# A two-layer decoder step: the second layer's S5 matrices built during the first layer's FFN, and S5 steps admitted by an account of VectorE's queue

## The chip, the cores and the metric

The kernel runs on one core of one Trainium2 chip. The metric is the device time of one execution in microseconds (us). TensorE is written PE here, VectorE DVE, ScalarE ACT, GpSimd POOL and SyncE SP, as the profile writes them.

## What is computed

Two layers (DEPTH 2), each over 288 tokens (256 of a prompt and 8 x 4 samples) of width 2048, cut from the reference:

```python
z = x @ w_in                                  # 2048 -> 3072: u (1024), cv (1024), cg (1024)
y5, h_re, h_im = _s5(u, h0_re, h0_im, ...)    # 64 groups x 16 channels, 64 complex states, a scan over positions
g5 = gelu(y5);  s5_out = g5 * sigmoid(g5 @ s5_w_glu)
c = cv * sigmoid(cg); c = causal_dwconv(c, width 31); c = silu(LN(c))
x = LN(ALPHA * x + concat(s5_out, c) @ w_out)
hup = causal_dwconv(x @ ffn_w_up, width 3);  gate, val = split(hup)
x = LN(ALPHA * x + (silu(gate) * val) @ ffn_w_down)
x = LN(ALPHA * x + sigmoid(x @ pe_w_gate) * (p @ pe_w))
```

Inside `_s5` the input matrix depends on weights alone: `bb = q * b` with q a complex number for each state, and powers of the state's factor `ab` times `c` give the output matrices. None of it depends on x.

## The kernel before

All large products run as three PE passes on 128x128 weight blocks (high part times high part, low times high, high times low; `run`, L369, L374, L375), one block after another in one fixed list. Every 8 blocks are one transfer of 512 KB (`wraw`, issued by SP). ACT makes the high part (`whi`, L195) and DVE the low part (`wlo`), two units of 8 blocks ahead of PE. A layer's phases are, in blocks: u0 (64), p0 to p7 (32 each, with v1 to v4 of 16 each after p1 to p4), g (64), o (256), then the FFN (up0, dn0, up1, dn1, up2, dn2) and the gate pg.

The S5 mixer works in 8 chunks of 8 groups beside the phases u0 to g of its own layer. For chunk c: `em` (the input matrix, built by four DVE operations in `make_e` from `sbt` and `sqb`) multiplies the inputs `ust` on PE (`inject`, output tile `bu`); DVE scans (`scan`, with tables `stb` and `sd` that POOL makes in `tables`); PE projects (`project`, tile `y`) with `om` and `tm`; `gelu` writes `y_d` to DRAM and `u<-y_d` brings it back as the input of phase g. `make_o` builds `om` from powers `pw`, and, through a PE product `kps`, a tile `kp`, a store `k_d` and a load `tm<-k_d`, the short-range matrix `tm`. `om` and `tm` of chunk c+1 wait for the projection of chunk c.

The convolution module runs beside it: after p_j, DVE fills `cbuf`, POOL stores it (`cb_d`), loads four shifted copies (`stack`), writes `cbuf` out (`out_dram<-cbuf`) and loads the next `cbuf`, which has one buffer. The convolution of stage j runs on PE after p_(j+1). In g, the first 32 blocks go by k, so that the block of k = 7 needs chunk 7 (`xs_g`, split to `xh` and `xl`).

Each engine executes its own queue in the order written. The S5 generators are asked for another step at every second block (`tick`). How far they may go is set by `self.rate` and by a clock `pe_t` that adds a fixed price for each block (369 ns), convolution tap (640 ns) and so on; a wait such as `wait(PJ_LAG)` counts on that clock. In `xs_g` the steps left are forced out, whatever the clock says.

```python
self.scan[2] = min(self.scan[2] + self.rate * (self.pe_t - self.pe_l), BANK)
while self.scan and self.scan[2] > 0 and self.step(self.scan): pass
...
while k not in gsplit:          # xs_g
    self.step(scan); self.run_timed(True); split_g(True)
```

## Time and profile before

| | us |
|---|---|
| three timed runs: median (lowest to highest) | 2794.82 (2787.64 to 2795.36) |
| the profiled execution | 2793.7 |
| its span, first to last instruction | 2791.9 |
| PE busy in it | 2684.0 (96%) |
| DVE, ACT, POOL busy | 1815.6, 1353.2, 304.3 |

PE is the engine that sets the time: every us in which it waits, or runs at its lower clock, is in the result, and other engines count only where PE waits for them. In the profile's slices PE is at 90% or more almost everywhere except in the two mixers, which lie at 0 to 300 us and at 1380 to 1680 us.

### The profile page before, as it was taken

The page shows a single profiled execution, that of the slowest core. Times are in us where ns is not written, and L with a number is a line of the kernel's source. Part 1 is how long each engine was busy: PE and PEld are TensorE (multiplying, and loading weights), DVE is VectorE, ACT ScalarE, POOL GpSimd, SP SyncE. Part 2 cuts the span into 40 slices and gives each one's busy share as a digit, 9 for nine tenths or more (in the row PEclk, how much of TensorE's full clock was granted, in tenths as well). Part 3 has the DMA queues.
Part 4 walks back from the last instruction along what each step waited for, and adds up shares of the span by engine and source line. Part 5 has one row for each costly group of instructions (what it writes and reads, how often), then busy time and mean ns, then how long its engine had stood idle before and what let it go on. Part 6 is the DMA issues. An engine that isn't in the chain of part 4 may idle for free. (4 is left out here: it accounts for less than half of the span.)

```text
span 2791.9 us, 57891 instructions
## 1 busy us (share of the span) xinstructions
PE 2684.0 (96%) x23696; PEld 2623.0 (94%) x23696; DVE 1815.6 (65%) x3017; ACT 1353.2 (48%) x2224; POOL 304.3 (11%) x923
## 2 busy tenths in 40 slices
PE   8889999999999999999889879999999999999997
PEld 7778999999999999999888769999999999999997
DVE  6875768664566456667778747676645664566686
ACT  3444547553455345536454435475534553455363
POOL 3442001000000000000115410010000000000000
PEclk9999999999999999999999999999999999999998
DMA  7887544554455544544468874445555455455543
GB/s 238 240 237 224 171 152 164 162 181 163 158 168 164 180 159 157 181 162 151 145 197 242 225 206 156 150 161 165 180 166 162 159 179 171 150 173 171 166 152 102
DMA packets 175609, 487.72 MB, mean 175 GB/s; under 512 B 37616, under 2 KB 61696, under 8 KB 175344
## 3 DMA queue, kind: packets, MB, share of 16 engines
q1 hardware_dynamic: 160832, 434.56, 48.6%
q0 software_dynamic: 14512, 49.47, 6.4%
q8 instruction: 186, 3.05, 0.4%
q14 instruction: 79, 0.65, 0.1%
HBM read 463.27 MB, written 20.68 MB: 173 GB/s over the span
## 5 line engine op out<-in xcount | busy, mean ns | idle before, releaser
L369 PE MATMUL acc<-xh,whi 128*128 128x288 f32 x4656 | 1389.3, 299 | 13.0 <-ACT xh L528 5.1
L374 PE MATMUL acc<-xl,whi 128*128 128x288 f32 x4357 | 1289.7, 296 | 0.6 <-DVE xl L140 0.2
L375 PE MATMUL acc<-xh,wlo 128*128 128x288 f32 x4357 | 1284.3, 295 | 0.5 <-issue 0.5
L195 ACT ACTIVATE whi<-wraw 128x1024 fp32r<-128x1024 f32 x766 | 791.4, 1050 | 350.5 <-PE acc L374 220.4
L140 DVE TENSOR_TENSOR wlo<-wraw,whi 128x1024 fp32r<-128x1024 f32 x766 | 918.6, 1223 | 28.6 <-issue 12.5
L369 PEld LDWEIGHTS acc<-xh,whi 128*128 128x128 f32 x4656 | 876.5, 188 | 20.5 <-ACT xh L528 5.4
L374 PEld LDWEIGHTS acc<-xl,whi 128*128 128x128 f32 x4357 | 821.4, 189 | 3.7 <-DVE xl L140 2.1
L375 PEld LDWEIGHTS acc<-xh,wlo 128*128 128x128 f32 x4357 | 823.8, 189 | 0.7 <-issue 0.7
L140 DVE SCALAR_TENSOR_TENSOR fo<-fe,parf,fo 128x304 f32<-128x304 f32 x352 | 188.2, 535 | 354.2 <-ACT fo L1250 347.9
L369 PE MATMUL acc<-hh,whi 128*128 128x288 f32 x1408 | 416.4, 296 | 0.0
L374 PE MATMUL acc<-hl,whi 128*128 128x288 f32 x1312 | 387.7, 296 | 0.0
L375 PE MATMUL acc<-hh,wlo 128*128 128x288 f32 x1312 | 387.4, 295 | 0.0
L369 PEld LDWEIGHTS acc<-hh,whi 128*128 128x128 f32 x1408 | 264.9, 188 | 0.1
L375 PEld LDWEIGHTS acc<-hh,wlo 128*128 128x128 f32 x1312 | 247.2, 188 | 0.0
L374 PEld LDWEIGHTS acc<-hl,whi 128*128 128x128 f32 x1312 | 247.0, 188 | 0.0
L1246 ACT ACTIVATE fe<-acc 128x256 f32<-128x256 f32 x176 | 67.6, 384 | 301.1 <-PE acc L375 301.1
L1256 POOL COPY fstage<-fe 128x9 f32<-128x9 f32 x176 | 42.2, 240 | 1035.3 <-ACT fe L1247 1024.5
L428 ACT ACTIVATE ln_q<-x 128x288 f32<-128x288 f32 x90 | 40.2, 446 | 221.0 <-DVE x L140 221.0
L140 DVE TENSOR_TENSOR x<-x,acc 128x288 f32<-128x288 f32 x64 | 29.1, 454 | 144.7 <-PE acc L375 144.7
L1250 ACT ACTIVATE fo<-fe,parf 128x304 f32<-128x304 f32 x176 | 113.0, 642 | 16.5
L1270 ACT ACTIVATE hh<-fth 128x288 fp32r<-128x288 f32 x88 | 39.2, 445 | 162.9 <-DVE fth L140 162.9
L140 DVE SCALAR_TENSOR_TENSOR x<-x,acc 128x288 f32<-128x288 f32 x64 | 29.0, 453 | 132.9 <-PE acc L375 132.9
(237 smaller groups left out, 2366.9 us busy)
## 6 DMA issues: line engine op xcount, KB each, us to landing
wraw<-in_wts_dram SPq DMA_DIRECT2D x776, 512.0 KB
stack<-cb_d POOLq DMA_DIRECT2D x56, 282.0 KB, 8.8
cw<-in_convw_dram POOLq DMA_DIRECT2D x16, 512.0 KB, 5.7
cbuf<-in_convi_dram POOLq DMA_DIRECT2D x16, 283.5 KB, 4.5
cb_d<-cbuf POOLq DMA_DIRECT2D x16, 283.5 KB, 4.0
out_dram<-cbuf POOLq DMA_DIRECT2D x16, 283.5 KB, 10.4
tm<-k_d SPq DMA_DIRECT2D x64, 64.0 KB
sbt<-in_s5b_dram SPq DMA_DIRECT2D x14, 256.0 KB
```

Of the source, the lines that this page charges most:

```text
L140: return f(out, *args, **kw)
L195: self.nc.scalar.activation(hi, self.raw[s], AF.Copy)
L369: nc.tensor.matmul(out, w[0], xh, start=first, stop=False)
L374: nc.tensor.matmul(out, w[0], xl, start=False, stop=False)
L375: nc.tensor.matmul(out, w[1], xh, start=False, stop=last)
L428: nc.scalar.activation(st["q"], v, AF.Square)
L1246: nc.scalar.activation(e[:, 2:2 + SEQ], acc[:, :SEQ], AF.Copy)
L1250: nc.scalar.activation(o[:, :w], e[:, 2:EW], AF.Identity, bias=self.prm("ffn_conv_b", m), scale=self.prm("ffn_conv_w2", m))
L1256: nc.gpsimd.tensor_copy(stage[:, z, :, 0], e[:, SEQ:EW:6])
L1270: nc.scalar.activation(hh[i], h, AF.Copy, scale=0.5)
```

## The change

In short: (1) `s5_early` builds the second layer's S5 matrices while the first layer's FFN runs, from dn0 on, and stores them in DRAM (`se`, `so`, `sk`); the second mixer loads them instead of building them. (2) An S5 step is admitted while the account of DVE's work (`dve_c`, 150 ns + 1.05 ns per element, twice that for the scan) is less than 1600 ns ahead of `pe_t`, in place of the rate. (3) Products are placed by that account: `e` is ready at `dve_c + E_LAG`, projections and `kps` wait until `dve_c + D_LAG` in place of `PJ_LAG`. (4) `pe_t` counts 400 ns for a block and 500 for a tap. (5) In the second layer a small POOL copy from `x32[0]` stands ahead of POOL's first S5 work.

```diff
-RATE = (1.05, 0.9)
-SETUP_RATE = 3
-BANK = 1400.0
+BACKLOG = 1600.0
+E_LAG = 2500.0
+K_LAG = 10000.0
+D_LAG = 1000.0
-PJ_LAG = 6000.0
+EARLY_LAG = 7000.0
+EARLY_RATE = 0.5
...
-            self.core.dve_t += 70.0 + n / 0.96
+            cost = 150.0 + (2.1 if name == "tensor_tensor_scan" else 1.05) * n
+            self.core.dve_c = max(self.core.dve_c, self.core.pe_t) + cost
...
-            self.scan[2] = min(self.scan[2] + self.rate * (self.pe_t - self.pe_l), BANK)
-            while self.scan and self.scan[2] > 0 and self.step(self.scan):
+            while self.scan and self.dve_c - self.pe_t < BACKLOG and self.step(self.scan):
...
-                self.pe_t += 369.0
+                self.pe_t += 400.0
...
+    def s5_load(self, l, c, pool, eng, which):
...
+    def s5_into(self, m, bt, qb):
+
+        V = self.V
+        shp = [P, 4, 2, ST]
+        V.tensor_tensor(m, qb, bt[:, :, 0:1].to_broadcast(shp), OP.mult)
+        V.tensor_tensor(qb, qb, bt[:, :, 1:2].to_broadcast(shp), OP.mult)
+        yield 1.0
+        V.tensor_tensor(m[:, :, 0], m[:, :, 0], qb[:, :, 1], OP.subtract)
+        V.tensor_tensor(m[:, :, 1], m[:, :, 1], qb[:, :, 0], OP.add)
+        yield 1.0
+
+    def s5_out(self, l, c, cc, bc, pw, bs, work):
...
+    def s5_steps(self, bs, pw, kp):
+
+        nc = self.nc
+        kps = self.ps.tile([P, 512], F32, tag="one", name="kps", bufs=1)
+        self.pe_t += 400.0
...
+    def s5_early(self, l, pool):
...
+        for c in range(S5C):
+            bt, qb = [self.s5_load(l, c, pool, eng, w) for w in "bq"]
+            cc, bc = self.s5_load(l, c, pool, eng, "o")
+            yield 1.0
+            yield from self.wait(EARLY_LAG)
+            m = work([P, 4, 2, ST])
+            yield from self.s5_into(m, bt, qb)
...
+            yield from self.wait(EARLY_LAG)
+            eng.dma_start(ed, m)
+            yield from self.s5_out(l, c, cc, bc, pw, bs, work)
+            yield from self.wait(EARLY_LAG)
+            self.s5_steps(bs, pw, kp)
+            eng.dma_start(od, pw[:, :, :, 1:5])
+            yield 1.0
+            yield from self.wait(EARLY_LAG)
...
+            eng.dma_start(kd, kp.rearrange("p k g o -> p (k g o)"))
+            self.early[c] = (ed, od, kd)
...
+            if early:
+                e = mp.tile([P, 4, 2, ST], F32, name="sbt", tag="sbt", bufs=1)
+                eng.dma_start(e, early[c][0])
+                return (e,)
...
+            if early:
+                kd, pk = early[c][2], cc
+            else:
+                yield from self.s5_out(l, c, cc, bc, pw, bs, work)
+                yield from self.until(self.dve_c + D_LAG)
...
-            self.at(BACK_LAG, back)
+            self.at(2000.0 if early else K_LAG, back)
...
-                state["e"] = c
+                self.timed.append((self.dve_c + E_LAG, lambda c=c: state.update(e=c)))
...
         def tail(c, us):
-            yield from self.wait(PJ_LAG)
+            yield from self.until(self.dve_c + D_LAG)
...
+        go0 = load_o(0, nc.gpsimd)
+        bt0 = None if early else self.s5_load(l, 0, mp, nc.gpsimd, "b")
+        if l:
+            G.tensor_copy(kp[:, 0, 0, 0:1], self.x32[0][:, 0:1])
...
-                    self.pe_t += 640.0
+                    self.pe_t += 500.0
...
+                if h == 0 and l + 1 < DEPTH:
+                    pre = self.start(self.s5_early(l + 1, fp), EARLY_RATE)
                 self.run(ph[f"dn{h}"], lambda k: (hh[k - j0], hl[k - j0]), ev_d0 if h == 0 else ev_dn)
```

`s5_load`, `s5_out` and `s5_steps` hold what `load_b`, `load_e`, `load_o` and `make_o` held. In the FFN, `eng` is SP.

Where instructions stand is decided by these accounts. Three places follow, each before and after.

The first is PE near the end of the first layer's mixer: the last projection `y` (chunk 7), before.

```order
L1108 MATMUL acc<-stack,cw 32x32 x4
L389 MATMUL y<-ust,tm 32x72 x4
L389 MATMUL y<-hin,om 32x72 x8
...
L389 MATMUL y<-hin,om 32x72 x8
L1105 MATMUL acc<-stack,cw 32x256 x4
L1108 MATMUL acc<-stack,cw 32x32 x4
L369 MATMUL acc<-xh_87,whi 128x288
```

It stands in the convolution ahead of p7. In the changed kernel it stands in g, between k = 6 (`xh_101`) and k = 7 (`xh_102`, which is made from this very chunk):

```order
L375 MATMUL acc<-xh_101,wlo 128x288
L389 MATMUL y<-ust,tm 32x72 x4
L389 MATMUL y<-hin,om 32x72 x8
...
L389 MATMUL y<-hin,om 32x72 x8
L369 MATMUL acc<-xh_102,whi 128x288
L374 MATMUL acc<-xl_118,whi 128x288
```

It moved 60 blocks later, and nothing is left between it and the block that needs it. Chunk 7's `kps` stands 14 blocks ahead of it.

The second is the same projection of the second layer. Before, it stands in p7, after 22 of its 32 blocks:

```order
L375 MATMUL acc<-xh_92,wlo 128x288
L389 MATMUL y<-ust,tm 32x72 x4
L389 MATMUL y<-hin,om 32x72 x8
...
L389 MATMUL y<-hin,om 32x72 x8
L369 MATMUL acc<-xh_93,whi 128x288
```

In the changed kernel it stands in the convolution ahead of p7, 22 blocks earlier:

```order
L1194 MATMUL acc<-stack,cw 32x32 x4
L389 MATMUL y<-ust,tm 32x72 x4
L389 MATMUL y<-hin,om 32x72 x8
...
L389 MATMUL y<-hin,om 32x72 x8
L1191 MATMUL acc<-stack,cw 32x256 x4
```

The third is POOL's queue where the second layer begins. Before, S5 comes first of all, and the convolution's transfers follow later:

```order
L745 DMA h_16275<-in_h_dram 128x512
L1038 MEMSET bsm 128x256
L1039 MEMSET kp 128x96
L1040 MEMSET hin 128x8
L790 DMA scc<-in_s5c_dram 128x128
L792 DMA sbc<-in_s5bs_dram 128x128
L776 DMA sbt<-in_s5b_dram 128x512
L1002 MEMSET om 128x1024
L886 TENSOR_TENSOR stb<-tix,fint 128x288
```

In the changed kernel the account admits no S5 step until after p0, and POOL has the first stage's transfers and the load of the second `cbuf` ahead of it:

```order
L1164 DMA stack<-cb_d 32x4x564 x4
L1166 DMA out_dram<-cbuf 128x567
L1201 DMA cbuf<-in_convi_dram 128x567
L866 DMA h_17177<-in_h_dram 128x512
L906 DMA sqb<-so_d_7902 128x512
L1125 COPY kp<-x_0_71 128x1
L1126 MEMSET bsm 128x256
L1127 MEMSET kp 128x96
L1128 MEMSET hin 128x8
L898 DMA sbt<-se_d_7901 128x512
L1085 MEMSET om 128x1024
L966 TENSOR_TENSOR stb<-tix,fint 128x288
```

On PE the first `bu` of the second layer follows 16 matmuls of the first convolution, 22 blocks later than before. POOL's tables of the second chunk now stand behind the load of the third `cbuf` (before: ahead of it), and in the first layer POOL's first tables stand behind the load of the second `cbuf` as well. The eight `kps` products of the second layer stand in dn0, up1 and dn1 of the first layer's FFN, 112 blocks apart.

## Rows read from the trace of the kernel before

**Rows 1.** Windows: us A:B, length, busy us of PE, PEld, DVE, ACT, POOL, clock, DMA

```profile
600.00:1220.00 620.00, 620.00 (x4652) 619.89 (x4651) 355.57 (x500) 289.57 (x444) 30.00 (x182) 1.00 0.52 167
1440.00:1680.00 240.00, 202.17 (x3298) 181.29 (x3299) 164.37 (x283) 98.38 (x189) 83.91 (x154) 0.92 0.80 223
```

**Rows 2.** PE's waits in 0 to 330 us: total, times, longest

```profile
PE bu L389 <- ACT em L815: 8.4, 7, 3.6
PE bu L389 <- DMA ust<-u_d: 6.0, 2, 3.4
...
PE y L389 <- DMA sqb<-q_d: 5.7, 1, 5.7
...
PE bu L389 <- issue: 1.6, 1, 1.6
```

**Rows 3.** PE's waits in 1360 to 1700 us

```profile
PE y L389 <- DMA wraw<-in_wts_dram: 7.6, 1, 7.6
...
PE lnp L510 <- DVE ln_dg L140: 7.2, 1, 7.2
PE y L389 <- ACT kp L858: 6.4, 2, 3.5
PE bu L389 <- DMA ust<-u_d: 5.2, 1, 5.2
PE acc L369 <- ACT xh L528: 5.1, 1, 5.1
PE y L389 <- DMA tm<-k_d: 3.1, 1, 3.1
PE bu L389 <- ACT em L815: 3.0, 3, 2.5
```

**Rows 4.** PE in order of time, second mixer: start, us, operation, wait before it

```profile
1455.53 1.08 PE L1105 MATMUL acc<-stack,cw 128*32 128x256 f32 x8 [7.40 <-DMA stack<-cb_d]
...
1485.37 1.21 PE L389 MATMUL bu<-ust,em 128*32 128x72 f32 x64
...
1580.38 2.15 PE L389 MATMUL bu<-ust,em 128*32 128x72 f32 x64 [5.17 <-DMA ust<-u_d]
...
1640.25 0.47 PE L389 MATMUL y<-ust,tm 128*32 128x72 f32 x8 [7.62 <-DMA wraw<-in_wts_dram]
```

**Rows 5.** DVE in order of time: the LayerNorm chain ahead of the second layer

```profile
1381.43 0.16 DVE L140 TENSOR_SCALAR ln_ne<-lnp 96x6 f32<-96x6 f32 x1 [1.85 <-PE lnp L459]
...
1387.70 0.87 DVE L140 SCALAR_TENSOR_TENSOR ln_dg<-ident,ln_n 96x288 f32<-96x288 f32 x1
```

**Rows 6.** DVE in order of time: the last LayerNorm's chain

```profile
2771.83 0.16 DVE L140 TENSOR_SCALAR ln_ne<-lnp 96x6 f32<-96x6 f32 x1 [1.78 <-PE lnp L459]
...
2774.36 0.45 DVE L140 SCALAR_TENSOR_TENSOR ln_dg<-ident,ln_n 96x288 f32<-96x288 f32 x1
```

**Rows 7.** POOL in order of time, 1380 to 1457 us

```profile
1383.61 0.68 POOL L886 TENSOR_TENSOR stb<-tix,fint 128x288 int32<-128x288 int32 x1
...
1444.53 0.56 POOL L1080 DMA_DIRECT2D out_dram<-cbuf  x1
1456.28 0.56 POOL L1115 DMA_DIRECT2D cbuf<-in_convi_dram  x1 [11.19 <-DMA out_dram<-cbuf]
```

**Rows 8.** The chain that ended last, 1640 to 1670 us: start, us, what

```profile
1649.15 3.19 DMA cb_d<-cbuf
...
1652.91 7.66 DMA stack<-cb_d
...
1660.59 7.21 DMA u<-y_d
...
1668.41 0.61 PE acc L369
```

**Rows 9.** DVE's groups by shape, 1400 to 1660 us: busy, mean ns, idle before

```profile
L140 DVE TENSOR_TENSOR sw<-scc,aP 128x512 f32<-128x512 f32 x16 | 10.7, 701 | 11.0 <-DMA scc<-in_s5c_dram 9.1 <-ACT em L815 1.9
...
L140 DVE TENSOR_TENSOR sw<-sqb,sbt 128x512 f32<-128x512 f32 x8 | 6.9, 867 | 17.3 <-DMA sqb<-q_d 9.1 <-DMA wraw<-in_wts_dram 8.2
```

**Rows 10.** PE's groups by shape, 1400 to 1680 us

```profile
L853 PE MATMUL kps<-pw,bsm 128*32 128x64 f32 x128 | 3.4, 224 | 0.0
```

**Rows 11.** DMA issues: queue, count, KB each, us to landing

```profile
y_d<-yw POOLq DMA_DIRECT2D x16, 144.0 KB, 3.5
...
sbt<-in_s5b_dram POOLq DMA_DIRECT2D x2, 256.0 KB, 4.9
```

**Rows 12.** ACT in order of time: one chunk's two `em` copies

```profile
1432.34 1.34 ACT L815 ACTIVATE em<-sw,mask 128x512 f32<-128x512 f32 x2 [3.87 <-DVE sw L140]
```

More of the change, by code (lines that the diff above doesn't have):

```diff
@@ L171, in __init__ @@
         self.nblk = DEPTH * NBLK
+        self.early = {}
     def stream_dma(self, upto):
@@ L281, in step @@
             return False
-        b[2] -= self.dve_t - t if b is self.scan else cost
+        b[2] -= cost
         return True
@@ L721, in stack_tile @@
         return mp.tile([P, 4, STW], F32, tag="stack", name="stack", bufs=1)
+    def s5_load(self, l, c, pool, eng, which):
+        a = self.a
+        if which == "b":
+            bt = pool.tile([P, 4, 2, ST], F32, name="sbt", tag="sbt", bufs=1)
+            eng.dma_start(bt, a["s5b"][l, c])
+            return bt
+        if which == "q":
+            qb = pool.tile([P, 4, 2, ST], F32, name="sqb", tag="sqb", bufs=1)
+            for q in range(4):
+                w = self.qd[l * NPAIR + 4 * c + q].rearrange("s g w -> (s g) w")
+                src = bass.AP(tensor=w.tensor, offset=w.offset, ap=[[P, 8], [0, CIN], [1, P]])
+                eng.dma_start(qb[:, q].rearrange("p i s -> p (i s)"), src)
+            return qb
+        cc = pool.tile([P, 4, 2, CIN], F32, name="scc", tag="scc", bufs=1)
+        eng.dma_start(cc, a["s5c"][l][:, 4 * c:4 * c + 4])
+        bc = pool.tile([P, 4, 2, CIN], F32, name="sbc", tag="sbc", bufs=1)
+        eng.dma_start(bc, a["s5bs"][l][:, 4 * c:4 * c + 4])
+        return cc, bc
@@ new lines, in s5_steps @@
+    def s5_steps(self, bs, pw, kp):
+        nc = self.nc
+        kps = self.ps.tile([P, 512], F32, tag="one", name="kps", bufs=1)
+        self.pe_t += 400.0
+        for i in range(2):
+            for q in range(4):
+                nc.tensor.matmul(kps[32 * q:32 * q + 32, :4 * CIN], bs[:, q, i].rearrange("p g c -> p (g c)"),
+                                 pw[:, q, i, 0:4].rearrange("p k o -> p (k o)"), start=(i == 0), stop=(i == 1),
+                                 tile_position=(0, 32 * q))
+        kv = kps[:, :4 * CIN].rearrange("p (k o) -> p k o", o=CIN)
+        for g in range(2):
+            nc.scalar.activation(kp[:, 3:7, g], kv, AF.Copy, scale=self.mask2[:, g:g + 1])
@@ L800, in load_u, with make_e @@
             return us
-        def make_e(bt, qb):
-            m = work([P, 4, 2, ST])
-            shp = [P, 4, 2, ST]
-            V.tensor_tensor(m, qb, bt[:, :, 0:1].to_broadcast(shp), OP.mult)
-            V.tensor_tensor(qb, qb, bt[:, :, 1:2].to_broadcast(shp), OP.mult)
-            yield 1.0
-            V.tensor_tensor(m[:, :, 0], m[:, :, 0], qb[:, :, 1], OP.subtract)
-            V.tensor_tensor(m[:, :, 1], m[:, :, 1], qb[:, :, 0], OP.add)
-            yield 1.0
+        def make_e(c, bt, qb=None):
+            m = bt
+            if not early:
+                m = work([P, 4, 2, ST])
+                yield from self.s5_into(m, bt, qb)
             mf = m.rearrange("p q i s -> p (q i) s")
@@ new lines, in make_o @@
+        def make_o(c, cc, bc=None):
+            if early:
+                kd, pk = early[c][2], cc
+            else:
+                yield from self.s5_out(l, c, cc, bc, pw, bs, work)
+                yield from self.until(self.dve_c + D_LAG)
+                while state["y"]:
+                    yield None
+                state["k"] = True
+                self.s5_steps(bs, pw, kp)
+                self.at(PS_LAG + 500.0, lambda: state.update(k=False))
+                yield None
+                k0 = kp[:, 3].rearrange("p g o -> p (g o)")
+                V.scalar_tensor_tensor(k0, self.eye, self.prm("s5_d", c), k0, op0=OP.mult, op1=OP.add)
+                kd = self.dp.tile([P, 7 * 2 * CIN], F32, tag="k_d", name="k_d", bufs=2)
+                G.dma_start(kd, kp.rearrange("p k g o -> p (k g o)"))
+                pk = pw[:, :, :, 1:5]
@@ L970, in gelu @@
             self.at(BACK_LAG, back)
-        state = {"i": -1, "p": -1, "e": -1, "o": -1, "y": False, "k": False}
+        early = self.early
+        state = {"i": -1, "p": -1, "e": -1, "o": -1, "y": False, "k": False, "t": -1}
         finals = []
@@ L1011, in main @@
                 yield from self.wait(PS_LAG)
+                while state["t"] < c:
+                    yield None
                 yield from scan(c, v, tb)
@@ L1025, in tail @@
         def tail(c, us):
-            yield from self.wait(PJ_LAG)
+            yield from self.until(self.dve_c + D_LAG)
             while finals:
@@ L1292, in ffn @@
                 nc.gpsimd.dma_start(a["ffno"][l][:, j0:j0 + n].rearrange("p j g b t -> p (j g) b t"), stage[:, :2 * n])
+                if h == 0 and l + 1 < DEPTH:
+                    pre = self.start(self.s5_early(l + 1, fp), EARLY_RATE)
                 self.run(ph[f"dn{h}"], lambda k: (hh[k - j0], hl[k - j0]), ev_d0 if h == 0 else ev_dn)
+                if last and l + 1 < DEPTH:
+                    assert pre not in self.bg
                 j0 += n
```

142 lines of the change are left out of this document (66 added, 76 removed).

## The prediction

> **What bounds the kernel now.** I read the busy time by stretches first, then PE's waits in each mixer, then the queues behind those waits. In the FFN PE is busy for 620.00 of 620 us at clock 1.00; in the second mixer it is busy for 202.17 of 240 us at a mean clock of 0.92 [rows 1]. So PE bounds the program, and only the mixers have time to give. From the FFN window a matmul takes 620 / 4652 = 0.133 us, so a block of three takes 0.40 us; I use that for every count of blocks. DVE is no bound: 164 of 240 us in the mixer, 356 of 620 in the FFN.
>
> PE's waits in the first mixer that S5 causes are 8.4 for `em`, 6.0 for `ust`, 5.7 and 1.6: 21.7 us [rows 2]. In the second mixer I count 7.6, 7.2, 6.4, 5.2, 5.1, 3.1 and 3.0 [rows 3] and 7.4 for the first `stack` [rows 4]: 45.0 us. The reader is to see that nearly all of them name S5 or its transfers: PE reaches a `bu` or `y` in its queue before the operands are there. After a wait PE runs at the lower of its two levels for a while: the same 64 `bu` matmuls take 1.21 us without a wait and 2.15 us after one of 5.17 [rows 4]. I charge 1.2 us for each wait over about 3 us (0.94 on the `bu` and a little on the blocks behind it).
>
> **Second layer: what goes.** The builders leave. DVE was occupied there with the first product of each builder for 10.7 + 6.9 us, and stood still ahead of these two groups for 11.0 + 17.3 us, because their loads were late [rows 9]; with the smaller operations of the builders this is what held `em`, `kp` and `tm` back. The eight `kps` products, 3.4 us of PE [rows 10], go to the FFN, where PE is fully busy: 3.4 off and 3.4 on, zero in the sum. The waits for `kp` (6.4) and most of those for `em` and `tm` go with them. The last projection stands 22 blocks earlier, ahead of p7, so that 60 blocks, 24 us, and a convolution lie between it and the block of k = 7. Before, 38 blocks (15.2 us) and a convolution lay there, and PE waited 5.1 us.
>
> **Second layer: what POOL's new order does.** The LayerNorm chain ahead of the layer lasts from 1381.43 to 1388.57, 7.1 us [rows 5], while POOL builds S5 tables beside it [rows 7]. The last LayerNorm's chain, with no POOL work, lasts 3.0 us [rows 6]. The first chain also holds two subtractions, which I estimate at 0.7 us together. With S5 behind the convolution's transfers the chain is left alone: the wait of 7.2 becomes 3.8.
>
> The price is the first chunk. POOL held the second `cbuf` load from the issue of `out_dram<-cbuf` at 1444.53 until 1456.28, because that store still read the one buffer [rows 7]. Behind this load now stand the state load, chunk 0's `sqb` and `sbt` and all S5 set-up. The first convolution could start at 1455.53 [rows 4], 0.75 us ahead of that point, and `bu` follows its second tap, perhaps 1 us on. But `sbt` then needs about 2 us of queue ahead of it (chosen: five short instructions and issues of some 0.3 to 0.6 us), 4.9 us to land [rows 11] and 1.3 us for its two `em` copies [rows 12]: 8.2 us after the hold ends. PE waits 8.2 - 0.25, so 8 us. Bounds: zero, if the store lands early, and 12, if the three loads queue behind the stack copies. Behind this `bu` stand the rest of the convolution and v1.
>
> The first `stack` wait of 7.4 stays. PE gets there 1.2 us sooner (no `bu` ahead of it) and 0.4 (no `kps`), DVE fills `cbuf` perhaps 1 to 2 us sooner: I keep 7. For chunk 1 POOL's tables stand behind the third `cbuf`, a hold like the 11.19 above. DVE will stand at that scan for some 7 us. Its low parts are made two units, 16 blocks or 6.4 us, ahead, so little of that reaches PE directly, but the projection behind it does: I take 5, between 0 and 8. For all other waits in the middle I take 3. At the end the chain store, `cbuf`, `cb_d`, `stack` stays (3.19 and 7.66 of it show in [rows 8]), and the second layer's last convolution will wait for it where 7.6 + 5.1 were waited before: I take 5, between 0 and 12.7.
>
> After the change: 3.8 + 7 + 8 + 5 + 3 + 5 = 31.8 us against 45.0. Waits over 3 us fall from eight to about five, 4 us of clock with rounding. **Second layer: -17.2 us.**
>
> The Trainium skill, page "DMA: Bandwidth & Descriptors", section "Issuing engines are not separate DMA queues", says that transfers issued from several engines share the same DMA engines, and that the issuing engine matters only for the short time that its sequencer needs. Taken alone it would leave the first chunk's loads as quick on POOL as on SP. POOL's 11.19 us here were a wait inside the queue, and by the row the choice of queue matters; this is the third rival below.
>
> **First layer.** Nothing is removed there. With `em` placed at `dve_c + 2500` and `ust` used later, the 21.7 us of waits lose their causes. New ones: the first tables stand behind the second `cbuf` load, so DVE stands at the first scan, of which I let 3 us reach PE; the first `stack` 2; others 2: 7 us. The clock gives back about 3.
>
> But S5 ends 60 blocks later. Chunk 7's projection stands directly ahead of the k = 7 block. Everything from it to `u<-y_d` and the split is then waited for by PE in full, and chunk 7's own `kps`, `k_d` and `tm` come only 14 blocks, 5.6 us, ahead. The nearest rows: in the second layer of before, from that projection at 1640.25 [rows 4] to PE's restart at 1668.41 [rows 8] are 28.2 us, with the last stack transfers among them. The store `y_d` (3.5) [rows 11] and the return (7.21) [rows 8] alone are 10.7. I take 20, about the middle of these two bounds, since `tm` and the wait for chunk 6 are in it too. With it 1 us of clock. First layer: -21.7 + 7 + 20 - 3 + 1 = **+3.3 us**, so about nothing: what S5 gains by patience it pays back in g.
>
> **FFN.** The two builder groups of [rows 9] are 17.6 us for eight chunks, 2.2 each; with the smaller operations I estimate three times that, some 6.6 us of DVE work per 112 blocks (45 us), on an engine that is 57% busy [rows 1], and on SP seven loads and three stores ahead of `wraw`. Cover: DVE's lead of 6.4 us and DMA at a share of 0.52. Loads are asked for 7 us ahead. I take 0; if DVE waits there as it did in the mixer (28.3 us in all [rows 9]) and its lead is used up, up to 28.
>
> **Sum.** 2793.7 - 17.2 + 3.3 = 2779.8; I say **2780 us**, against the profiled execution's own 2793.7. The median of the runs shown, 2794.82, is 1.1 us (0.04%) above it, far inside what a measurement here can tell: less than 0.3%, 8.4 us, I call the same.
>
> **Rivals.**
> *The new waits do not come.* If POOL's hold hides, `em` (8), chunk 1 (5) and the rest (3) go, and the first layer's tail shrinks to its lower bound of 10.7 (9 less): 2780 - 16 - 9 = 2755; with the second tail gone too (5), 2750. For it: DVE has the builders off and SP fewer loads. Against it: the order of POOL's queue. 0.20.
> *Layer 1 pays in full.* The tail costs 28.2 and half of the 21.7 in the middle stays, since DVE's work there is not reduced: 2780 + 8 + 11 = 2799. For it: the first layer's S5 ran at DVE's pace all along. Against it: the account prices DVE's operations about as they last. 0.19.
> *The page's rule.* POOL's queue costs issue time alone: 8 less, 2772. Against it, the row of 11.19. 0.07.
> *Slower: the FFN.* DVE stands in the FFN for the early loads as in the mixer; where one wait exceeds its lead of 6.4 us, `wlo` is late and PE, with nothing in reserve, stops. The single wait of 8.2 in [rows 9] is above that point. All 28.3 us: 2808. Against it: DMA's share is 0.52 there, 0.80 in the mixer. 0.10.
> That the change would not do what it says is excluded by the order of PE's queue: the `kps` products stand in the FFN.
>
> **Chances.** The forecast holds 0.44, with its own range of 2767 to 2793 (the `em` term from 0 to 12, the tail some 6 us either way). Under 2786 lie three quarters of it (0.33), the first rival (0.20) and the rule (0.07): faster 0.60. The same: 0.11 of the forecast and 0.12 of the second rival: 0.23. Slower: 0.07 of the second rival and 0.10: 0.17. The range of 2750 to 2803 leaves out the FFN case and half of the first rival.
>
> **What would show it.** In the profile after, the second layer's chain ahead of `ln_dg` lasts about 3.7 us; PE's largest wait at a `bu` stands early in the second layer with `em` or a load as its cause, and POOL's `cbuf` just ahead of the S5 loads; no wait names `kp` there. In the first layer one long wait at `xh<-u` in g, 15 to 28 us, directly behind the last `y`. In 600 to 1220 us PE stays at 620. The prediction is wrong if the tail of layer 1 is short, if the first `bu` of layer 2 does not wait, or if the FFN loses time.

## The result, and the profile after

| | us |
|---|---|
| changed kernel, six timed runs: median (lowest to highest) | 2812.63 (2804.47 to 2816.73) |
| kernel before, six runs beside them | 2795.09 (2787.64 to 2799.75) |
| ratio, with its 95% interval | 1.0061 (1.0042 to 1.0080) |
| the profiled execution of the changed kernel, its span | 2807.88, 2806.1 |

The change makes the kernel slower by 0.6%, 17 us. The forecast was 2780 us with a range of 2750 to 2803: the time lies above the range, and on the side that had 0.17.

I cut each profile at three points of PE's queue: the start of the last convolution matmul of the first layer, of the first `lnp` matmul of the LayerNorm ahead of the second layer, and of the last convolution matmul of the second layer. In the changed kernel they lie at 315.1, 1412.0 and 1688.8 us. They give, for every profile of this study (us; the second profile of before is that of `before_again`, below):

| profile | first mixer | middle, with the FFN | second mixer | rest | ratio of timed runs |
|---|---|---|---|---|---|
| before, two profiles | 285.2, 289.1 | 1092.8, 1092.4 | 299.2, 295.8 | 1114.7, 1114.7 | 1 |
| changed | 315.1 | 1096.9 | 276.8 | 1117.3 | 1.0061 |
| `l1_before` | 289.1 | 1098.8 | 278.1 | 1117.3 | 0.9965 |
| `l1_setup` | 304.1 | 1098.8 | 278.5 | 1114.7 | 1.0027 |
| `l1_admit` | 301.9 | 1097.5 | 278.5 | 1118.8 | 0.9987 |
| `back4500` | 323.2 | 1096.1 | 280.5 | 1118.8 | 1.0096 |
| `pool_tables_first` | 310.1 | 1099.1 | 283.8 | 1119.0 | 1.0060 |
| `l1_tm_early` | 289.1 | 1096.4 | 278.6 | 1117.2 | 0.9967 |
| `tm_early` | 318.0 | 1098.3 | 282.7 | 1117.2 | 1.0060 |
| `setup_tm_early` | 312.3 | 1096.3 | 277.5 | 1115.8 | 1.0036 |
| `setup_b4500` | 302.5 | 1097.8 | 275.9 | 1117.3 | 1.0027 |
| `setup_b8000_tm` | 301.7 | 1098.0 | 279.1 | 1114.5 | 1.0010 |
| `early_only` | 291.1 | 1099.6 | 276.5 | 1118.9 | 0.9967 |
| `l2_account_only` | 294.1 | 1092.0 | 333.5 | 1114.3 | 1.0152 |
| `early_tm` | 292.6 | 1098.1 | 271.2 | 1116.2 | 0.9934 |
| `early_tm_gate` | 291.6 | 1098.7 | 266.5 | 1117.3 | 0.9918 |

The two profiles of before differ by 4 us in a mixer, so a single cell is good to about that. The changed kernel loses 28 us in the first mixer, gains 21 in the second, and gives some 4 to the middle and 2.6 to the rest.

The windows between these points, laid out as in [rows 1], split that into waits and work. First mixer, before and changed, then the second mixer, before and changed:

```profile
0.00:285.20 285.20, 249.65 (x3630) 220.34 (x3633) 196.16 (x402) 113.66 (x219) 106.91 (x200) 0.96 0.80 237
```

```profile
0.00:315.10 315.10, 256.89 (x3629) 225.79 (x3633) 200.08 (x407) 115.63 (x223) 109.67 (x200) 0.92 0.74 215
```

```profile
1378.00:1677.20 299.20, 252.34 (x3714) 228.07 (x3712) 210.53 (x376) 132.91 (x245) 100.22 (x183) 0.91 0.74 208
```

```profile
1412.00:1688.80 276.80, 242.76 (x3586) 227.03 (x3584) 152.32 (x250) 125.11 (x208) 81.75 (x171) 0.94 0.75 218
```

A window less PE's busy time is PE's waiting. In the first mixer the waits grew by 22.7 us (35.5 to 58.2), and PE was busy 7.2 us longer for the same matmuls, at a mean clock of 0.92 where it had been 0.96. (Before's second profile has the same 35.5 us of waits, but is busy for 253.6: against it the growth is 3.3.) In the second the waits fell by 12.8 us (46.9 to 34.0) and the busy time by 9.6, of which 3.4 are the `kps` products that went to the FFN. In the middle it is PE's busy time that grew, from 1088.9 to 1093.4.

PE's waits of the changed kernel in 0 to 330 us (total, times, longest), the answer to [rows 2]:

```profile
PE acc L369 <- ACT xh L528: 16.3, 2, 8.7
PE y L389 <- DMA tm<-k_d: 10.3, 3, 6.0
PE acc L412 <- ACT cvo L1196: 6.6, 1, 6.6
PE acc L365 <- DMA wraw<-in_wts_dram: 5.7, 1, 5.7
PE acc L1191 <- DMA stack<-cb_d: 5.5, 1, 5.5
PE acc L369 <- issue: 4.1, 1, 4.1
PE y L389 <- DMA sqb<-q_d: 3.7, 1, 3.7
PE kps L792 <- DVE bsm L143: 2.6, 2, 2.0
PE bu L389 <- ACT em L925: 2.4, 2, 2.1
```

Without the first weight load (5.7, which before has too) these rows are 51.5 us. And in 1390 to 1730 us, the answer to [rows 3]:

```profile
PE bu L389 <- ACT em L925: 8.8, 6, 6.7
PE y L389 <- issue: 6.7, 2, 4.5
PE acc L1191 <- DMA ust<-u_d: 5.0, 1, 5.0
PE lnp L510 <- DVE ln_dg L143: 3.6, 1, 3.6
```

The FFN's window, the answer to [rows 1], and the stretch of the first mixer that lost most:

```profile
600.00:1220.00 620.00, 619.36 (x4738) 616.82 (x4737) 390.42 (x608) 297.15 (x486) 42.44 (x199) 1.00 0.58 183
...
60.00:120.00 60.00, 40.42 (x561) 35.53 (x560) 36.51 (x64) 20.68 (x39) 26.69 (x40) 0.83 0.70 192
```

And the instructions that the reading rests on, in order of time (start, us, operation, wait before it):

```profile
82.21 0.56 POOL L1201 DMA_DIRECT2D cbuf<-in_convi_dram  x1 [11.39 <-DMA out_dram<-cbuf]
...
85.13 0.69 ACT L974 ACTIVATE stb<-stb 128x576 f32<-128x576 int32 x1 [18.36 <-POOL stb L967]
...
85.85 1.42 DVE L143 TENSOR_TENSOR sw<-bu,stb 128x576 f32<-128x576 f32 x2 [16.51 <-ACT stb L974]
...
267.81 0.47 PE L389 MATMUL y<-ust,tm 128*32 128x72 f32 x8 [5.99 <-DMA tm<-k_d]
294.01 0.61 PE L369 MATMUL acc<-xh,whi 128*128 128x288 f32 x1 [7.57 <-ACT xh L528]
307.85 0.61 PE L369 MATMUL acc<-xh,whi 128*128 128x288 f32 x1 [8.75 <-ACT xh L528]
...
1483.65 0.54 POOL L898 DMA_DIRECT2D sbt<-se_d  x1
...
1486.55 0.68 ACT L974 ACTIVATE stb<-stb 128x576 f32<-128x576 int32 x1 [20.57 <-POOL stb L967]
...
1490.09 0.46 PE L389 MATMUL bu<-ust,em 128*32 128x72 f32 x4 [6.68 <-ACT em L925]
```

The second mixer reads as forecast: the LayerNorm wait 3.6, the first `bu` waits for `em`, no `kp`. The first mixer does not. Its three late waits are the end that was forecast at 20: 5.99 ahead of chunk 6's projection, directly behind p7, then 7.57 and 8.75 in g, at the blocks of k = 6 and k = 7, 22.3 us in all. But some 30 us of waits lie ahead of them, where the forecast had 7 new ones beside some 8 that before has too and that it let stand, and in 60 to 120 us PE also ran at a mean clock of 0.83. In that stretch POOL's first tables stand behind the held `cbuf` load (11.39), ACT's sine stands behind POOL for 18.36 us and VectorE's first scan behind ACT for 16.51, with `whi`, `cvo` and `wlo` of the convolution and the weights behind them in the two queues. That was my first explanation, and it fell.

### The profile page after: what moved, and what is told of

It reads as the page before. It is cut to its first block, busy times and chain, and to the rows that moved or that the text cites. A ratio compares the mean times of both kernels' runs of the same rounds, so it can differ in the third digit from the quotient of the medians.

```text
span 2806.1 us, 57940 instructions
## 1 busy us (share of the span) xinstructions
PE 2687.9 (96%) x23696; PEld 2631.4 (94%) x23696; DVE 1803.8 (64%) x3017; ACT 1354.7 (48%) x2224; POOL 298.9 (11%) x913
## 4 chain that ended last, share of the span: by engine, by line
PE 82%; DMA 7%; DVE 4%; issue 3%; POOL 2%; ACT 1%; SPq 1%; ACTq 0%; DVEq 0%; POOLq 0%
PE acc L369 26%; PE acc L374 24%; PE acc L375 24%; DMA out_dram<-cbuf 2%; PE acc L351 2%; PE acc L371 2%; PE acc L365 1%; DVE wlo L143 1%; DMA tm<-k_d 1%; DMA wraw<-in_wts_dram 1%; PE acc L1191 1%; DVE sw L143 1%; PE y L389 1%; DMA cb_d<-cbuf 1%; DMA scc<-in_s5c_dram 0%
## 5 line engine op out<-in xcount | busy, mean ns | idle before, releaser
L369 PE MATMUL acc<-xh,whi 128*128 128x288 f32 x4656 | 1391.8, 299 | 26.3 <-ACT xh L528 16.3
L198 ACT ACTIVATE whi<-wraw 128x1024 fp32r<-128x1024 f32 x766 | 792.7, 1052 | 333.5 <-PE acc L374 204.2
L1332 ACT ACTIVATE fe<-acc 128x256 f32<-128x256 f32 x176 | 67.6, 384 | 294.1 <-PE acc L375 294.1
```

The source lines that it names most:

```text
L198: self.nc.scalar.activation(hi, self.raw[s], AF.Copy)
L369: nc.tensor.matmul(out, w[0], xh, start=first, stop=False)
L1332: nc.scalar.activation(e[:, 2:2 + SEQ], acc[:, :SEQ], AF.Copy)
```

## The experiments

The kernels come from one source: that of the changed kernel with the admission, the places and the prices of before as switches for each layer. With every switch off its five queues are row for row those of the changed kernel. BY_RATE brings back the rate, OLD_PLACE the places (PJ_LAG, `e` at once, BACK_LAG for `tm`), OLD_PRICE 369 and 640 ns.

```diff
         if self.scan:
-            while self.scan and self.dve_c - self.pe_t < BACKLOG and self.step(self.scan):
-                pass
+            if self.by_rate:
+                self.scan[2] = min(self.scan[2] + self.rate * (self.pe_t - self.pe_l), BANK)
+                while self.scan and self.scan[2] > 0 and self.step(self.scan):
+                    pass
+            else:
+                while self.scan and self.dve_c - self.pe_t < BACKLOG and self.step(self.scan):
+                    pass
```

### Which part of the change costs

**`l1_before`: the first mixer as before, all else as changed.**

```diff
-BY_RATE = ()
-OLD_PLACE = ()
-OLD_PRICE = ()
+BY_RATE = (0,)
+OLD_PLACE = (0,)
+OLD_PRICE = (0,)
```

> The changed kernel, with everything in the first layer's mixer put back as it was before: admission by the rate, PJ_LAG in place of the account, 369 and 640 ns in the clock. Its instructions then stand in the first mixer as before, and from the FFN on as in the changed kernel. Theory (the loss lies in the first mixer alone, from the way S5 steps are admitted there): the 29.9 us of the first mixer come back, 2812.6 - 29.9 = 2783, range 2776 to 2788, faster than before by 0.3 to 0.6%. Rival (the early build costs time in the FFN, about as much as it gives in the second mixer): 2795 or more, and PE under 615 busy us in 600 to 1220 us.

2784.5 us, ratio 0.9965 (0.9952 to 0.9977); the first mixer took 289.1 us in place of 315.1. The theory holds: the loss lies in the first mixer and goes with its admission, places and prices. The FFN's cost, the rival, stays: in 600 to 1220 us PE was busy for 619.2 us.

**`early_only`: the early build alone**, both mixers as before. **`l2_account_only`: the account in the second layer alone**, the first mixer as before and no early build.

```diff
-BY_RATE = (0,)
-OLD_PLACE = (0,)
-OLD_PRICE = (0,)
+BY_RATE = (0, 1)
+OLD_PLACE = (0, 1)
+OLD_PRICE = (0, 1)
```

```diff
-                if h == 0 and l + 1 < DEPTH:
-                    pre = self.start(self.s5_early(l + 1, fp), EARLY_RATE)
```

The first diff makes `early_only` out of `l1_before`, the second `l2_account_only`.

> The early build of the second layer's matrices alone: both mixers have the admission, the places and the prices of before, and the second mixer loads se, so and sk. Theory (the second mixer's gain of 21 to 22 us comes from the builders' leaving): the second mixer takes 278 to 286 us, 2783 to 2792 us in all. Rival (the gain comes from the account, which sets S5 behind the convolution's transfers and leaves the LayerNorm chain alone): the second mixer takes 290 us or more, 2795 us or more in all.

> The first mixer as before, no early build, and the second mixer, which builds its matrices itself again, by the account and its places. Theory (the account costs wherever the matrices are built in the mixer: S5 then ends in g, 32 blocks later than before): the second mixer takes 310 us or more in place of 299, 2803 us or more in all. Rival (the account is good for the second layer, and it was the start of the program that made it bad in the first): the second mixer takes 290 us or less, 2788 us or less.

`early_only`: 2783.4 us, 0.9967 (0.9956 to 0.9977), the second mixer 276.5 us. `l2_account_only`: 2834.55 us, 1.0152 (1.0137 to 1.0167), the second mixer 333.5 us in place of 297.5 (the mean of before's two). So the early build brings the whole gain of the second mixer; with it the account brings and costs nothing there (276.8; by the timed runs `early_only` and `l1_before` have 0.9967 and 0.9965), and without it the account costs 36 us. PE's waits of `l2_account_only` in 1380 to 1730 us show the same faces as the first mixer of the changed kernel:

```profile
PE acc L386 <- ACT xh L545: 20.8, 3, 10.5
PE y L406 <- DMA tm<-k_d: 16.9, 5, 5.5
```

The account loses wherever a mixer builds its own matrices.

### What in the account costs

**`pool_tables_first`: POOL's order alone.**

```diff
-M0_LAG = 8000.0
+M0_LAG = 0.0
```

> The changed kernel with M0_LAG 0 in place of 8000 ns. The queues of PE, VectorE and SP stay row for row as in the changed kernel; on POOL, in the first layer, the first tables and the initial state move ahead of the store, the copies and the load of the second cbuf, and ACT's first sine moves with them. Theory (the set-up's loss is POOL's hold of the tables behind the cbuf load, and the two queues that stand behind it): ACT's wait of 18.4 us and VectorE's of 16.5 us are gone, the first mixer gets about as much back as from the whole set-up by rate (11 us), 2798 to 2804 us. Rival (what costs is that the whole set-up is late, whatever POOL's order): 2808 to 2817 us, the waits at cvo and stack stay or are replaced by waits for the chunk's matrices.

2808.66 us, 1.0060 (1.0043 to 1.0077): the rival. The waits of 18.4 and 16.5 us are gone, and others stand in their place. In this kernel's order of time and waits (0 to 330 us):

```profile
85.39 0.69 DVE L152 TENSOR_TENSOR sw<-sqb,sbt 128x512 f32<-128x512 f32 x1 [10.33 <-DMA sqb<-q_d]
```

```profile
PE acc L386 <- ACT xh L545: 16.1, 2, 8.6
PE y L406 <- DMA tm<-k_d: 15.2, 4, 5.2
```

VectorE now waits for the `sqb` load behind the same late set-up. A row of 18.36 us named the engine that came last, not the cause.

**`l1_setup`: the set-up by the rate of before, the rest by the account.**

```diff
-SETUP_BY_RATE = False
+SETUP_BY_RATE = True
```

> The changed kernel, but the set-up of the first layer's S5, up to POOL's first tables and initial state, is admitted by the rate of before (3), and only what follows by the account. POOL's first tables then stand ahead of the load of the second cbuf; the last projection stays in g, directly ahead of the block of k = 7. Theory (two losses of about the same size: the late set-up, which puts POOL's tables behind the held cbuf load, and the late end in g): the first one goes, the second stays: ACT's wait of 18.4 us at stb and VectorE's wait of 16.5 us behind it are gone, waits in g stay near 20 us, 2790 to 2800 us. Rival (the pace after the set-up is what costs, set by the account and the places by dve_c): within 5 us of the changed kernel, 2807 to 2817 us, with the waits at other places.

2800.49 us, 1.0027 (1.0014 to 1.0040): 9.5 us less than the changed kernel by their ratios, half a us above the theory's range and 6.5 below the rival's. The theory's two waits are gone (VectorE has one of 11.0 for a later chunk's tables), and 18.7 us are left in g. The windows of the first 60 us tell why (DVE busy is the third figure): the changed kernel, `l1_setup`, and before's queues in `before_again`.

```profile
0.00:60.00 60.00, 54.29 (x281) 44.70 (x282) 30.03 (x110) 14.92 (x30) 11.50 (x33) 1.00 0.72 239
```

```profile
0.00:60.00 60.00, 52.25 (x330) 41.86 (x331) 38.82 (x129) 19.55 (x41) 23.51 (x47) 1.00 0.71 238
```

```profile
0.00:60.00 60.00, 50.81 (x262) 40.36 (x262) 40.17 (x128) 19.55 (x41) 23.23 (x47) 1.00 0.69 230
```

In this stretch VectorE has room, and the account lets it stand idle: 30.03 us of work in place of 39 to 40. In the stretches 120 to 180 and 180 to 240 us it is busy for 46 to 50 us of 60 in the changed kernel and in `before_again`, so what was not done early has little room left there. What remains of the loss in `l1_setup` are its waits (0 to 330 us):

```profile
PE acc L386 <- ACT xh L545: 18.7, 2, 11.0
...
PE y L406 <- DMA tm<-k_d: 6.4, 2, 3.7
```

**`l1_admit`: the whole first layer by the rate, places and prices as changed.**

```diff
-BY_RATE = ()
+BY_RATE = (0,)
```

> The changed kernel, but the whole first layer's S5 is admitted by the rate of before (3 in the set-up, then 1.05); the places of its products (E_LAG, D_LAG, K_LAG) and the prices of the clock (400 and 500 ns) stay as changed. The last projection then stands at block 384 of the layer, ahead of the last convolution's neighbours, where it stood at 412 in the changed kernel and 352 before. Theory (admission is the cause, the places are not): the first mixer takes 285 to 295 us, 2778 to 2793 us in all. Rival (the products' places and the longer lags cost the time): the first mixer stays above 305 us, 2803 us or more.

2790.59 us, 0.9987 (0.9975 to 0.9999), within the theory's 2778 to 2793; this profile lies 8 us above the median, so its first mixer of 301.9, above the 285 to 295 that the theory had for it, says less than the ratio. Admission is the larger part: 20.7 us of the 26.8 between the changed kernel and `l1_before` (both by their ratios, times 2794). The rest shows in the waits of `l1_admit` and in its order of time:

```profile
PE y L406 <- DMA tm<-k_d: 15.3, 5, 4.3
...
PE acc L386 <- ACT xh L545: 10.6, 1, 10.6
```

```profile
111.85 0.54 POOL L960 DMA_DIRECT2D k_d<-kp  x1 [5.46 <-DVE kp L152]
...
123.14 5.13 SPq L192 DMA_DIRECT2D wraw<-in_wts_dram  x2
...
128.36 3.01 SPq L973 DMA_DIRECT2D tm<-k_d  x4
...
137.25 0.47 PE L406 MATMUL y<-ust,tm 128*32 128x72 f32 x8 [3.77 <-DMA tm<-k_d]
```

The store `k_d` was issued at 111.85, its load only at 128.36: with K_LAG 10000 the load is written behind weight transfers in SP's queue.

**`l1_tm_early`: that load 6 us of the clock earlier**, the projection where it was.

```diff
-K_LAG = 10000.0
+K_LAG = 4000.0
...
-                self.at(LOAD_LAG, lambda: state.update(o=c))
+                self.at(LOAD_LAG + (0.0 if early else 6000.0), lambda: state.update(o=c))
```

> The kernel l1_admit with the load of tm written 6 us of the clock earlier (K_LAG 4000 in place of 10000) while the projection stays where it was (its own lag is 6000 longer): the last projection stands at block 384 in both. Theory (with K_LAG 10000 the loads of tm stand behind one weight transfer more in SP's queue, so the projections wait for them): PE's waits at y for tm fall from 15.3 us to under 5, the first mixer takes 290 to 295 us in place of 301.9, 2779 to 2786 us in all. Rival (the store of kp or the lateness of VectorE is what makes tm late): the waits stay over 10 us, 2788 to 2793 us.

2783.24 us, 0.9967 (0.9953 to 0.9981); the same load was issued at 119.77, 8.6 us sooner, and took 1.80 us to issue:

```profile
119.77 1.80 SPq L973 DMA_DIRECT2D tm<-k_d  x4
```

```profile
PE y L406 <- DMA tm<-k_d: 1.6, 1, 1.6
```

The theory holds, and this kernel is as good as `l1_before` with the prices and the other places of the change: with the load of `tm` this early, E_LAG, D_LAG, 400 and 500 ns cost nothing that the timed runs show.

**`tm_early` and `setup_tm_early`: the same edit in the changed kernel and in `l1_setup`.**

> The changed kernel with the first layer's load of tm written 6 us of the clock earlier (K_LAG 4000, and 6000 more until the projection), nothing else. Theory (three parts of the first mixer's loss add up: the late set-up some 11 us, the late loads of tm some 10 us, the late end the rest): PE's waits at y for tm fall from 10.3 us to under 4, the last projection stays in g, 2801 to 2807 us. Rival (the end in g is where all lateness of the layer comes out, and an earlier tm only moves the wait there): 2809 us or more, with more than 20 us of waits at xh.

> The kernel l1_setup (set-up by the rate of before, the rest by the account) with the load of tm written 6 us of the clock earlier. Theory (the parts add up): 2800.5 less 6 to 10 us, 2790 to 2795 us, and the rest of the way to 2784 is the wait in g, which stays near 18 us. Rival (the pace of the account after the set-up is a further cost of its own): 2797 us or more.

2812.74 us, 1.0060 (1.0041 to 1.0080), and 2804.21 us, 1.0036 (1.0021 to 1.0051): the rival in both. Under the account the waits at `y` for `tm` go as well, and nothing is won: in `tm_early` the waits in g grow to 20.5 and those for `stack` to 12.7.

```profile
PE acc L386 <- ACT xh L545: 20.5, 2, 11.8
```

So the parts don't add up one by one; I had expected that they would. While S5 as a whole is late, its last chunk sets the end, and a wait removed ahead of it comes out there.

### Is the limit only too narrow?

**`back4500`: BACKLOG 4500 in the first layer.**

```diff
-            while self.scan and self.dve_c - self.pe_t < BACKLOG and self.step(self.scan):
+            while self.scan and self.dve_c - self.pe_t < BACKLOG[self.lay] and self.step(self.scan):
```

> The changed kernel with BACKLOG 4500 in place of 1600 ns in the first layer alone: the account admits S5 steps while VectorE's queue is 4.5 us ahead of the clock. The first tables then stand ahead of the second cbuf load, and the last projection at block 396 in place of 412, 16 blocks (6.4 us) earlier. Theory (the account is only set too tight for a layer that builds its matrices): most of the 29.9 us come back, the tail in g shrinks from 22 to about 10 us, 2782 to 2795 us. Rival (steps let in earlier only fill VectorE's queue, so that wlo comes late instead): 2803 us or more, with PE's waits at wlo or cvo instead.

2821.05 us, 1.0096 (1.0074 to 1.0117): slower still, and not at `wlo` or `cvo` as the rival had it. PE's products stand earlier in its queue, but the set-up is hardly earlier (VectorE busy for 30.91 us of the first 60), so PE reaches them before their operands:

```profile
PE bu L406 <- ACT em L942: 20.4, 7, 9.7
PE y L406 <- DMA tm<-k_d: 16.5, 3, 7.9
```

```profile
176.53 8.98 SPq L973 DMA_DIRECT2D tm<-k_d  x4
...
188.05 0.47 PE L406 MATMUL y<-ust,tm 128*32 128x72 f32 x8 [7.87 <-DMA tm<-k_d]
...
190.98 0.76 DVE L152 TENSOR_TENSOR hin<-sw 128x252 f32<-128x252 f32 x2 [9.61 <-PE y L406]
```

The three rows are one chain: the projection waits for `tm`, VectorE waits for the projection at `hin`, and the next chunk's matrices stand behind VectorE.

**`setup_b4500`: `l1_setup` with that limit. `setup_b8000_tm`: set-up by the rate, limit 8000, and `tm` early.**

> The kernel l1_setup (set-up of the first layer's S5 by the rate of before) with BACKLOG 4500 in place of 1600 ns in the first layer: the last projection then stands at block 388 in place of 410. Theory (after the set-up it is the narrow limit of 1600 ns that makes the layer end late; back4500 was slow because its set-up was still late): waits at xh fall from 18.7 to about 10 us, the whole like l1_admit, 2786 to 2795 us. Rival (a wider limit only fills VectorE's queue, as in back4500, whatever the set-up): 2800 us or more.

> The changed kernel with all three suspects taken out of the first layer and nothing else put back: set-up by the rate of before, BACKLOG 8000 ns behind it, the load of tm 6 us of the clock earlier. The last projection stands at block 380. Theory (late set-up, narrow limit and late tm are the whole loss, and each has to go before the others pay): like l1_before and l1_tm_early, 2780 to 2788 us, y waits for tm in the first mixer under 5 us. Rival (there is a further cost in the account's places, E_LAG and D_LAG, or in the prices of 400 and 500 ns): 2792 us or more.

2800.48 us, 1.0027 (1.0011 to 1.0043), and 2794.53 us, 1.0010 (0.9998 to 1.0023). With the set-up early, 4500 in place of 1600 changes nothing in the time: waits at xh fall from 18.7 to 10.3 as expected, those for `tm` rise from 6.4 to 16.0; the time is at the rival's bound. With all three suspects gone the kernel is 14 us better than the changed one, but 12 short of `l1_tm_early`, though its projections stand within 4 blocks of that kernel's. The rival's range came, but not its reason, since `l1_tm_early` has the account's places and prices too. In its order of time:

```profile
176.81 1.29 DVE L152 TENSOR_TENSOR sw<-scc,aP 128x512 f32<-128x512 f32 x2 [7.72 <-DMA scc<-in_s5c_dram]
...
176.81 0.26 ACT L787 ACTIVATE pw<-scc 128x64 f32<-128x64 f32 x1 [6.35 <-DMA scc<-in_s5c_dram]
...
181.37 0.61 PE L392 MATMUL acc<-xh,wlo 128*128 128x288 f32 x1 [11.54 <-DVE wlo L152]
```

The wide limit lets the builder be written before its `scc` is there; both engines stand in front of that load with `whi` and `wlo` behind them. The account counts what VectorE does and no wait of it, so I read the three limits as one trade: a narrow limit starves the chain and a wide one blocks the queue. The wide end of it is argued, not shown: in 60 to 300 us VectorE waits for `scc` under the rate as well:

```profile
DVE sw L152 <- DMA scc<-in_s5c_dram: 24.5, 6, 7.7
```

```profile
DVE sw L152 <- DMA scc<-in_s5c_dram: 19.5, 4, 6.3
```

The first row is of `setup_b8000_tm`, the second of `l1_tm_early`. What differs more is how much reaches PE: its waits for `wlo` are 18.0 us in the first and 6.8 in the second. Why the rate keeps them small stays open, and a limit between 1600 and 8000 with `tm` and the set-up early was not run.

### What the early build is worth

**`early_tm`: `early_only` with the second layer's load of `tm` 5 us of the clock earlier. `early_tm_gate`: that, with the two first loads and the small POOL copy of the change ahead of the second layer's S5.**

```diff
-            self.at(BACK_LAG if old else 2000.0 if early else K_LAG, back)
+            self.at(2000.0 if early else BACK_LAG if old else K_LAG, back)
...
-                self.at(LOAD_LAG, lambda: state.update(o=c))
+                self.at(LOAD_LAG + (5000.0 if early else 0.0), lambda: state.update(o=c))
```

```diff
-        if not old:
+        if not old or l:
             go0, bt0 = first()
             if l:
                 G.tensor_copy(kp[:, 0, 0, 0:1], self.x32[0][:, 0:1])
```

> The kernel early_only with the second layer's load of tm written 5 us of the clock earlier (2000 in place of BACK_LAG, and 5000 more until the projection); PE, VectorE, ACT and POOL stay row for row as in early_only, SP alone differs. Theory (a load in SP's queue waits for the weight transfers ahead of it): PE's waits at y for tm in the second mixer fall from 12.3 us to under 4, 2772 to 2779 us. Rival (tm has one buffer, so the earlier load waits in SP's queue for the projection before, and holds up weights behind it): 2781 us or more, with waits of PE, ACT or VectorE for wraw in the second mixer.

> The kernel early_tm with the changed kernel's small POOL copy from x32[0] ahead of POOL's S5 work in the second layer (and the two first loads ahead of it): POOL's tables then wait until the LayerNorm's result is there. Theory (POOL's tables beside the LayerNorm chain make it 4 us longer): the wait ahead of the second layer falls from 7.6 to about 3.6 us, 4 us less than early_tm, 2768 to 2775 us. Rival (the tables then come late for the first scan, and PE waits there for what it won): within 2 us of early_tm.

2777.44 us, 0.9934 (0.9917 to 0.9950), and 2773.66 us, 0.9918 (0.9900 to 0.9936): both beat both kernels. The theories hold, but other waits grew beside the ones that went. Two waits of `early_only` in 1380 to 1730 us:

```profile
PE y L406 <- DMA tm<-sk_d: 12.3, 3, 6.2
PE lnp L527 <- DVE ln_dg L152: 7.6, 1, 7.6
```

In `early_tm` the first is gone and the LayerNorm's stays, while `stack` grew from 3.8 to 9.6 (1370 to 1710 us), and the second mixer won 5 of the 12. And `early_tm_gate`, where PE's queue is the same row for row, halves the LayerNorm wait; the 4 us between its time and that of `early_tm` are not clear of the two intervals:

```profile
PE lnp L527 <- DVE ln_dg L152: 3.6, 1, 3.6
```

**`before_again`: before's own queues, from this source.** All switches to before, and no early build.

> The kernel before once more, from the changed kernel's source with every switch put back and no early build: its five queues are row for row those of before. Theory (the first mixer's 289 to 294 us in the profiles of l1_before, early_only and the others, against 285.2 in the one profile of before, is how one execution differs from another): the ratio holds 1.000, and this profile's first mixer lies anywhere from 284 to 293 us. Rival (something of the early build, or of the changed source, slows the first mixer though its queues are the same): 1.000, and the first mixer within 2 us of 285.2 with waits at bu for ust near 6 us.

2792.44 us, 0.9993 (0.9978 to 1.0008). Its first mixer took 289.1 us, with 12.0 us of waits at `bu` for `ust` where the first profile had 6.0 [rows 2]: the theory, one execution differs from another by some 4 us there. The early build's kernels have 289.1 to 292.6. So of its gain of some 21 us in the second mixer 9 reach the ratio of `early_only`: 3.4 are the `kps` products, now in the FFN (the middle grew by 4 to 7 us), some 3 lie in the rest (1116 to 1119 in place of 1114.7), and up to 3 in the first mixer. In the rest, `early_only` and the changed kernel have a wait of 1.1 us for `cvo` just behind the cut that before doesn't have, and PE is busy for 1.8 to 3.5 us more with the same matmuls. Why that wait comes, and what makes the middle longer than 3.4, stays open.

## Why the prediction was wrong

**What bounds the kernel** was read rightly: nearly all that moved lies in the mixers, and it is PE's waits and the clock behind them.

**Second layer, -17.2: right.** Against the mean of before's two profiles the second mixer gained 20.7 us; 3.4 of these are the `kps` products, which the forecast moved to the FFN at no gain, so 17.3 stand against 17.2. The waits fell by 12.8 us by the windows above, forecast 13.2. Of the single terms some are luck. LayerNorm 3.8, measured 3.6; first `em` 8, measured 6.7; first `stack` 7, measured 5.0 (at the load of `ust`, which PE meets at the same point); the tail 5, measured about 2. Chunk 1's 5 did not come: PE meets its `bu` and its `y` without a wait. The 6.7 us at `y` lie in the middle of the projections of chunks 2 and 4, at 1544.4 and 1581.2 us; their cause, "issue", is none that the profile shows. What I had not asked is which part of the change earns the gain. I credited POOL's new order with 3.4 and charged it 8; by `early_only` the early build alone reaches the same 276.5 us.

**The Trainium skill's rule** on issuing engines (page "DMA: Bandwidth & Descriptors", section "Issuing engines are not separate DMA queues"), the third rival, did not come: the first `bu` waited 6.7 us for work behind POOL's held queue. Its load `sbt` was issued there only at 1483.65, and landed 3.7 us later; ACT, which makes `em`, stood 20.57 us for POOL's first table and came to `em` behind two `whi`, 2 us after the landing. SP's queue gave a second case: the same load of `tm`, written ahead of two weight transfers, was issued 8.6 us sooner and took 13.7 us of waits away. Where a load stands in its issuer's queue counted more here than the short time of the issue.

**FFN, 0: right** at the scale of the forecast. VectorE took 35 us more in 600 to 1220 us [rows 1], PE stayed at 619.4, so the slower rival did not come either. VectorE did stand there for the early build's loads of `sqb`, 9.4 us in five waits, but the longest was 4.0, under its lead of 6.4. (Of the 28.3 us that this rival charged, 8.2 were put down to `wraw` and 1.9 to ACT [rows 9]: not all were late loads of S5.) The middle grew by 4.3, of which 3.4 are the `kps` that the forecast put there.

**First layer, +3.3: this is the step that failed, in its middle and in its clock.** It said that the 21.7 us of waits "lose their causes", that 7 of new waits come in the middle and 20 at the end, and that the clock gives 2 back. That is +5.3 us of waits and -2 of work; measured against the same profile it was +22.7 and +7.2. The end was right at 22.3, though it came as three waits and not as one long one. Ahead of it the waits were 15 us longer than forecast. The clock, which was to give 2 us back, cost 7.2, or 3.3 against before's second profile.

The new places did take the waits at `bu` away (2.4 for `em` is left, and none for `ust` is in the list), but I priced the account as if it only moved products. It also withheld work: about 9 us of VectorE's work in the first 60 us, where VectorE had room. And K_LAG, 10000 where BACK_LAG was 7000, which I gave no price at all, put the loads of `tm` behind weights. By the timed runs, undone one after another: the set-up 9.5 us, the rest of the admission 11.2, the load of `tm` 5.6, together 26.3 of the 26.8 that `l1_before` gives back. The third number has an uncertainty of its own size; that the waits fell from 15.3 to 1.6 us is in the traces. Which wait carries the 11.2 is not shown.

**The rival "layer 1 pays in full"** (2799) had the sign and the place, and argued from VectorE's pace; it was 14 us short, since it let half of the old 21.7 stay where the waits were new ones. The first rival (the new waits don't come) came true for the second layer's chunk 1 and tail alone.

## What to carry to other kernels

A limit on how far one engine's queue may run ahead costs time if it holds work back where that engine has room: here a limit of 1.6 us left VectorE idle at the start of the mixer, and the set-up alone was worth 9.5 us. An account that counts what the engine does and not what it waits for does not see this; whether a wide limit fails for the same reason stayed open. When work moves out of a crowded stage, give it its own trial: the early build alone gained 0.3% where the whole change lost 0.6%, and with two small edits beside it 0.8%. A long wait names the instruction that came last; before it is taken for a cause, move that instruction alone and see whether the time follows.

## What the runs showed of the hardware

The issue of the same four `tm` transfers on SP took 1.80 us, 3.01 us and 8.98 us in the three rows above; the DMA engines' share around them was 0.81 (115 to 125 us), 0.95 (120 to 132) and 0.89 (170 to 190). So the same four issues can take five times as long, and they hold up what is written behind it in SP's queue. The length does not follow that share (the longest stands at 0.89, not at 0.95), and what sets it I did not try.

The wait for the LayerNorm chain ahead of the second layer was 7.6 us with POOL's tables beside it and 3.6 behind the gate, with the same instructions on VectorE and PE. The Trainium skill, page "SBUF — State Buffer", section "Who interferes with whom", describes a port pair that VectorE and GpSimd share and that one of them holds for a whole instruction; these two runs agree with it, and give 4 us as its price in this chain. In the kernel before, the chain's second TENSOR_SCALAR on `ln_ni`, of 96x3 elements, lasts 0.96 us beside a MEMSET of POOL of 0.97 that starts 0.04 us ahead of it; the same instruction lasts 0.17 us behind the gate.
